# Interleaving two float32 tensors: transfer rows of 32 KiB instead of 16 KiB, with two buffers for each stream

## The chip, the cores and the metric

The kernel runs on one core of one Trainium2 chip. The metric is the device time of one launch in microseconds. Runs of one kernel mostly agree within about 0.3%.

A ratio below is the mean time of one kernel's fast runs over that of the kernel before in the same rounds on the same chip, so it is not quite the ratio of the medians that are quoted beside it.

## The reference

```python
batch, seq, dim = 32, 256, 1024           # x and y: float32, 33.6 MB each
result = np.zeros((batch, seq, dim * 2), dtype=np.float32)
result[..., 0::2] = x
result[..., 1::2] = y
```

No arithmetic is done. 67.1 MB are read and 67.1 MB written.

## The kernel before

Both inputs are treated as flat arrays and cut into tiles of 128 partitions x `WL` elements. SyncE issues the loads; VectorE copies x into the even columns and y into the odd columns of an output tile; ScalarE's queue issues the store. The tile list ends in a *taper*: smaller and smaller tiles. A *row* is the contiguous stretch that a transfer moves for one partition; the profile lists each row's move as a *packet*. An issue is the instruction that starts a transfer, a landing its end.

```python
WL = 4096          # load row: 4096 x 4 B = 16 KiB for each partition
WS = 2048          # store row: 2 x 2048 x 4 B = 16 KiB
xpool = ctx.enter_context(tc.tile_pool(name="xp", bufs=3))
ypool = ctx.enter_context(tc.tile_pool(name="yp", bufs=3))
opool = ctx.enter_context(tc.tile_pool(name="op", bufs=6))

lwidths = [WL] * (total // P // WL - 1) + [2048, 1024, 512, 256, 256]
for lw in lwidths:
    xtile = xpool.tile([P, WL], fp32, name="xtile")[:, :lw]
    ytile = ypool.tile([P, WL], fp32, name="ytile")[:, :lw]
    xs = dataclasses.replace(xf, offset=start, ap=[[lw, P], [1, lw]])
    ...
    nc.sync.dma_start(out=xtile, in_=xs)
    nc.sync.dma_start(out=ytile, in_=ys)
    soff = 0
    while soff < lw:
        width = min(WS, lw - soff)
        otile = opool.tile([P, 2 * WS], fp32, name="otile")[:, : 2 * width]
        ...
        nc.vector.tensor_copy(out=otile[:, 0::2], in_=xsub)
        nc.vector.tensor_copy(out=otile[:, 1::2], in_=ysub)
        nc.scalar.dma_start(out=os_, in_=otile)
        soff += width
    start += P * lw
```

## Time and profile before

| | kernel before |
|---|---|
| time, median of 4 | 319.75 us (319.66 to 320.22) |
| span in the profile | 317.6 us |
| bytes moved | 134.2 MB |
| VectorE busy | 24% of the span |
| 16.8 MB (eight transfers) in the steady part, called a *period* | 38.90 us, 431.3 GB/s |
| loads / stores | 40 / 35 |

The engines that move data are busy all the time, so the question for any change is only: at which rate do they run, and for how long are they not busy at the start and at the end? The prediction below shows the lines that say so. The period is read from the chain of waits, in order of time (start, length, what):

```profile
77.21 38.84 DMA xtile<-in_x_dram
...
116.11 38.84 DMA xtile<-in_x_dram
...
232.81 31.51 DMA xtile<-in_x_dram
```

(232.81 - 77.21) / 4 = 38.90 us. The texts on record have 38.89, from one window.

### The profile page before, as it was taken

The page shows a single profiled execution, that of the slowest core. Times are in us where ns is not written, and L with a number is a line of the kernel's source. Part 1 is how long each engine was busy: PE and PEld are TensorE (multiplying, and loading weights), DVE is VectorE, ACT ScalarE, POOL GpSimd, SP SyncE. Part 2 cuts the span into 40 slices and gives each one's busy share as a digit, 9 for nine tenths or more (in the row PEclk, how much of TensorE's full clock was granted, in tenths as well). Part 3 has the DMA queues.
Part 4 walks back from the last instruction along what each step waited for, and adds up shares of the span by engine and source line. Part 5 has one row for each costly group of instructions (what it writes and reads, how often), then busy time and mean ns, then how long its engine had stood idle before and what let it go on. Part 6 is the DMA issues. An engine that isn't in the chain of part 4 may idle for free.

```text
span 317.6 us, 285 instructions
## 1 busy us (share of the span) xinstructions
DVE 76.8 (24%) x70; POOL 0.2 (0%) x4
## 2 busy tenths in 40 slices
DVE  0522112222022221122220222202222202221130
POOL 0000000000000000000000000000000000000000
DMA  8999999999999999999999999999999999999997
GB/s 293 429 396 429 429 431 429 429 429 437 437 435 433 433 429 429 429 429 429 429 431 429 429 429 435 437 437 430 431 431 429 431 429 429 429 432 427 421 423 285
DMA packets 10802, 134.24 MB, mean 423 GB/s; under 512 B 1200, under 2 KB 1712, under 8 KB 2608
## 3 DMA queue, kind: packets, MB, share of 16 engines
q1 hardware_dynamic: 5760, 67.11, 50.0%
q10 hardware_dynamic: 5040, 67.11, 49.4%
q14 instruction: 2, 0.02, 0.0%
HBM read 67.11 MB, written 67.11 MB: 423 GB/s over the span
## 4 chain that ended last, share of the span: by engine, by line
DMA 94%; issue 3%; SPq 1%; DVE 1%
DMA xtile<-in_x_dram 82%; DMA ytile<-in_y_dram 12%; SPq L51 0%; DVE otile L69 0%; SPq L50 0%; DVE otile L68 0%
## 5 line engine op out<-in xcount | busy, mean ns | idle before, releaser
L68 DVE COPY otile<-xtile 128x2048 f32<-128x2048 f32 (+3 forms) x35 | 38.4, 1134 | 118.4 <-issue 94.4
L69 DVE COPY otile<-ytile 128x2048 f32<-128x2048 f32 (+3 forms) x35 | 38.4, 1134 | 117.9 <-DMA ytile<-in_y_dram 117.9
L90 POOL MEMSET const-bfloat16-1.0<- 128x1 bf16 x1 | 0.1, 102 | 0.0
L90 POOL MEMSET const-uint8-127<- 128x1 uint8 x1 | 0.1, 101 | 0.0
L90 POOL MEMSET const-float32-0.0<- 128x1 f32 x1 | 0.1, 99 | 0.2 <-issue 0.2
L90 POOL MEMSET const-float32-1.0<- 128x1 f32 x1 | 0.1, 98 | 0.0
## 6 DMA issues: line engine op xcount, KB each, us to landing
out_dram<-otile ACTq DMA_DIRECT2D x31, 2048.0 KB, 19.5
xtile<-in_x_dram SPq DMA_DIRECT2D x15, 2048.0 KB, 38.8
ytile<-in_y_dram SPq DMA_DIRECT2D x15, 2048.0 KB, 38.8
xtile<-in_x_dram SPq DMA_DIRECT2D x1, 1024.0 KB, 36.4
ytile<-in_y_dram SPq DMA_DIRECT2D x1, 1024.0 KB, 34.0
out_dram<-otile ACTq DMA_DIRECT2D x1, 1024.0 KB, 9.2
xtile<-in_x_dram SPq DMA_DIRECT2D x1, 512.0 KB, 29.0
ytile<-in_y_dram SPq DMA_DIRECT2D x1, 512.0 KB, 30.2
```

The lines of the kernel that those rows point to most:

```text
L68: nc.vector.tensor_copy(out=otile[:, 0::2], in_=xsub)
L69: nc.vector.tensor_copy(out=otile[:, 1::2], in_=ysub)
L90: nc = _bacc.Bacc("TRN2", target_bir_lowering=False, num_devices=1)
```

## The change

Its intent is to make all rows twice as long. The on-chip memory stays the same: 3 + 3 + 6 buffers of 16 KiB for each partition become 2 + 2 + 2 of 32 KiB, 192 KiB in both. The taper's pieces double as well.

```diff
-    WL = 4096
-    WS = 2048
+    WL = 8192
+    WS = 4096
@@
-    xpool = ctx.enter_context(tc.tile_pool(name="xp", bufs=3))
-    ypool = ctx.enter_context(tc.tile_pool(name="yp", bufs=3))
-    opool = ctx.enter_context(tc.tile_pool(name="op", bufs=6))
+    xpool = ctx.enter_context(tc.tile_pool(name="xp", bufs=2))
+    ypool = ctx.enter_context(tc.tile_pool(name="yp", bufs=2))
+    opool = ctx.enter_context(tc.tile_pool(name="op", bufs=2))
@@
-    lwidths = [WL] * (total // P // WL - 1) + [2048, 1024, 512, 256, 256]
+    lwidths = [WL] * (total // P // WL - 1) + [4096, 2048, 1024, 512, 512]
```

(A dead branch and an unused counter are removed too.)

More of the change, by code (lines that the diff above doesn't have):

```diff
@@ L33 @@
     fp32 = mybir.dt.float32
-    xpool = ctx.enter_context(tc.tile_pool(name="xp", bufs=3))
-    ypool = ctx.enter_context(tc.tile_pool(name="yp", bufs=3))
-    opool = ctx.enter_context(tc.tile_pool(name="op", bufs=6))
-    lwidths = [WL] * (total // P // WL - 1) + [2048, 1024, 512, 256, 256]
+    xpool = ctx.enter_context(tc.tile_pool(name="xp", bufs=2))
+    ypool = ctx.enter_context(tc.tile_pool(name="yp", bufs=2))
+    opool = ctx.enter_context(tc.tile_pool(name="op", bufs=2))
+    lwidths = [WL] * (total // P // WL - 1) + [4096, 2048, 1024, 512, 512]
     assert sum(lwidths) == total // P
     start = 0
-    k = 0
     for lw in lwidths:
@@ L63 @@
             ysub = ytile[:, soff : soff + width]
-            if False:
-                nc.gpsimd.tensor_copy(out=otile[:, 0::2], in_=xsub)
-                nc.gpsimd.tensor_copy(out=otile[:, 1::2], in_=ysub)
-            else:
-                nc.vector.tensor_copy(out=otile[:, 0::2], in_=xsub)
-                nc.vector.tensor_copy(out=otile[:, 1::2], in_=ysub)
+            nc.vector.tensor_copy(out=otile[:, 0::2], in_=xsub)
+            nc.vector.tensor_copy(out=otile[:, 1::2], in_=ysub)
             nc.scalar.dma_start(out=os_, in_=otile)
-            k += 1
             soff += width
```

## The prediction

> **What bounds the kernel now.** I read the page's first two parts, then the DMA groups, then a table of windows, then the chain of waits, and last what the load queue waited for.
>
> ```profile
> DVE 76.8 (24%) x70; POOL 0.2 (0%) x4
> ...
> DMA  8999999999999999999999999999999999999997
> GB/s 293 429 396 429 429 431 429 429 429 437 437 435 433 433 429 429 429 429 429 429 431 429 429 429 435 437 437 430 431 431 429 431 429 429 429 432 427 421 423 285
> DMA packets 10802, 134.24 MB, mean 423 GB/s; under 512 B 1200, under 2 KB 1712, under 8 KB 2608
> ...
> q1 hardware_dynamic: 5760, 67.11, 50.0%
> q10 hardware_dynamic: 5040, 67.11, 49.4%
> ```
>
> VectorE works a quarter of the span; the 16 DMA engines are busy in every slice, and the rate is flat except in the first and last slice. The packets tell how a row travels: 40 loads and 35 stores, each 128 rows plus 16 more, give 40 x 144 = 5760 and 35 x 144 = 5040. So a row is one packet, 16 KiB ones too.
>
> The windows (columns: stretch, length, VectorE busy, POOL busy, clock, DMA share, GB/s) give the rate of the steady part and of the edges:
>
> ```profile
> 3.00:8.46 5.46, 0.00 (x0) 0.00 (x0) 1.00 0.97 411
> ...
> 38.27:77.21 38.94, 9.46 (x8) 0.00 (x0) 1.00 1.01 431
> ...
> 288.70:296.00 7.30, 1.23 (x1) 0.00 (x0) 1.00 0.99 423
> 296.00:302.25 6.25, 1.23 (x1) 0.00 (x0) 1.00 1.00 421
> ...
> 312.70:315.00 2.30, 0.29 (x1) 0.00 (x0) 1.00 1.01 403
> 315.00:317.60 2.60, 0.00 (x0) 0.00 (x0) 1.00 0.15 55
> ```
>
> The chain of waits, in order of time (start, length, what), repeats one load every 38.9 us; its last load is tiny and slow:
>
> ```profile
> 38.31 38.84 DMA xtile<-in_x_dram
> ...
> 304.54 8.17 DMA ytile<-in_y_dram
> ```
>
> In a period of 38.89 us go eight transfers of 2.097 MB: 8 x 2.097 / 38.89 = 431.4 GB/s, or 4.86 us for each when alone. A load lands 38.8 us after its issue, eight times 4.86: four loads were in flight, each getting half the rate. That is a queue, not a latency. Hence the chain's 94% DMA means "the transport is full", not "a load comes late". The sum: 134.2 MB / 431.4 GB/s = 311.1 us of transport; the 2.57 MB moved by 8.46 us put its start at 2.5 us; the data ends about 315.3; then the last landing and the end, 2.3 us. That leaves 317.6 - 2.5 - 311.1 - 2.3 = 1.7 us lost, nearly all in the tail with its short rows. The measured time, 319.79, is 2.2 above the span.
>
> The load queue's own waits show that buffers are not the point:
>
> ```profile
> SPq L50 <- DMA xtile<-in_x_dram: 126.5, 14, 9.9
> SPq L51 <- DMA ytile<-in_y_dram: 121.9, 14, 9.4
> ```
>
> A load issue waits for an earlier load, not for a copy. The instruction order says why: completions are counted on eight semaphores in rotation, and in the steady part the x load of tile k must wait until that of tile k-2 has landed. The third x and y buffers are therefore scarcely used today; stores hold four of those semaphores.
>
> **What the Trainium skill says.** Four places, all on the page "DMA: Bandwidth & Descriptors". "Where 436 GB/s comes from" puts the ceiling of the 16 engines at 435 GB/s; the trace agrees, 431 in the steady part (single slices of 437 are packets booked in the slice in which they end). "Why small descriptors are slow (HBM only)" states a fixed overhead of about 3 cycles per packet; the trace agrees in direction, 421 to 423 GB/s where loads have rows of 8 and 4 KiB. "Queues, rings and completion order" says that each engine takes its queues in turn, one packet at a time; the trace agrees: the last y load, 128 KB, took 8.17 us, because each of an engine's 8 small rows waited behind a store's row. "Latency and other measured facts" reports that row pitches of 2 MiB and more in HBM cut the rate by a fifth to a half, and 512 KiB by only 3%; here the store pitch grows from 32 to 64 KiB, far below, and nothing in this trace shows such a loss.
>
> **The change part by part.** *Rows.* 24 loads and 19 stores in place of 40 and 35: (24 + 19) x 144 = 6192 packets instead of 10800. Per engine a 2.097 MB transfer is 8 rows, 131072 bytes, in 4861 ns; at the skill's ceiling it would be 4819. So at most 42 ns per transfer (5 ns a row) is overhead; doubled rows halve it: 21 of 4861, 0.43%, of 311.1 us = 1.3 us if all of the gap is per row or per transfer. It may be something else that does not halve; I take -0.9 us.
>
> *VectorE.* From 128x1024 at 695 ns and 128x2048 at 1225 ns the slope is 0.518 ns per element, so 128x4096 takes 1225 + 2048 x 0.518 = 2286 ns (estimate). 30 of these, 2 of 1225, 2 of 695 and 4 of 429 make 74.1 us instead of 76.8: beside the transport, worth nothing.
>
> *Start.* The first pair of loads is 8.4 MB instead of 4.2, so the first store is issued near 25 us instead of 14.6. But four loads, 16.8 MB or 39 us of transport, are issued at once, so the engines are full meanwhile: 0.
>
> *Steady part, with two buffers each.* I walk it with 9.72 us for a 4.194 MB transfer alone and 19.45 when shared. x0 lands at 8.46 + 4.86 = 13.3, y0 at 23.0, so store 0a is issued at 25.3 and 0b at 29.9. Sharing starts at about 26.8: x1 lands 38.7, y1 58.2, x2 77.6, y2 97.1, and stores 0a, 0b, 1a, 1b at 46.2, 65.7, 85.1, 104.6. Store 2a needs only y2's copy (its buffer came free at 85.1): issued 97.1 + 2.3 = 99.4, 5.2 us before 1b ends. The second half needs the buffer of 1b: copies 104.6 to 109.2, then store 2b is issued and y4's load too, x4's at 106.9, while x3 is in flight until 116.5 and y3 behind it. So the next period looks the same: the store queue is refilled 5.2 us (first half) and about 15 us (second half) ahead, and the load queue always holds a load or two. And should one run dry, the other takes the whole rate. Cost 0.
>
> *Tail.* Its pieces are twice as large, and only two output buffers are left. Continuing the walk, y6 lands near 252.7. Then loads with 16 and 8 KiB rows compete with 32 KiB store rows and get a third, then a fifth: x7 267.3, y7 281.9, x8 294.1; store 6b ends 286.5, store 7 298.7; y8 lands 300.2. Only loads are left then for some 4 us, just enough: y8's rest, x9, y9 and x10 are 1.5 + 1.2 + 1.2 + 0.6 us of work. Store 8 is issued at 301.5, runs from 303 to 308, and its buffer is what the copies of tile 10 wait for: about 309.4 with the landing. Store 9 fills until 310.4, store 10 begins near 311.8, tile 11's copies wait for store 9's landing, and the last store is issued near 312.8. The 256 KB last store of today lands in 3.2 us; one of 512 KB needs 0.6 more: 316.6, and 1.3 to the end of the span: 317.9. This is today's 317.6 + 0.3; the holes (some 1.4 us between stores 9 and 10, and 1 before 11) replace the losses of today's tail. I add 0.3 because such waits stack up late rather than early.
>
> *Sum.* 317.6 + 0.3 (tail) + 0.3 (its risk) - 0.9 (rows) = 317.3 of span; plus 2.2: 319.5 us.
>
> **Rivals.** First: two output buffers starve the store queue. For it: VectorE must wait for a store's landing before every copy, and refilling is only 5.2 us ahead. Against: stores share the engines with queued loads, so starving one queue costs nothing until both are empty. If both ran dry for 2 us in each of 7 periods: +14, 334. I give it 3%.
>
> Second: long rows move the HBM itself to another rate, by the pitch of 64 KiB or by turns between reading and writing 32 KiB at a time. For a gain: 423 to 431 from shorter to longer rows. Against: 431 is within 0.9% of the ceiling, so no more than 134.2/435.2 = 308.4 us can come of it, 2.7 less than now; the whole would be 317.1, not 2% faster. For a loss: nothing in this trace; 3% of loss would be 329. I give that 3%.
>
> Third: the tail with rows of 2 KiB behind rows of 32 KiB. Each engine's 8 rows of a small load can wait 8 x 1.2 = 9.7 us if a store of 32 KiB rows is in flight; if y8 or y9 lands after the stores have run out, the engines stand idle for the copy, the issue and the start of the next store, 3 us a time. For it: the 8.17 us above, and that my walk has only 0.3 us to spare at 303. Against: today's tail has the same proportions and lost under 2 us. It would make 321 to 323.
>
> **Range and chances.** The good end is the full row gain and today's tail, 318.2 or a little less; the bad end the third rival, 322.5. Range 317.7 to 322.5. Two per cent are 6.4 us: faster would need more than the ceiling leaves, slower one of the first two rivals. Faster 0.01, same 0.94, slower 0.05.
>
> **What would show it.** Right: 6194 packets; steady windows of 431 to 434 GB/s; 128x4096 copies near 2290 ns; a 4 MB load landing some 30 to 40 us after its issue; load issues waiting for copies or stores instead of earlier loads; the loss confined to the last 20 us. Wrong: a slice in the middle below 420 GB/s, both queues idle at once, a steady rate below 428, or packets split so that the count stays at 10800.

## The result, and the profile after

318.78 us (median of 4, 318.45 to 319.12) against 319.75; ratio 0.997, 95% interval 0.9956 to 0.9984. That is 0.3% faster: within 2%, clear of noise, and 0.7 us below the predicted 319.5.

The page of the changed kernel, its busy line, its rates and its packets:

```profile
DVE 73.5 (23%) x38; POOL 0.2 (0%) x4
...
GB/s 332 406 456 394 427 435 439 423 448 414 456 410 456 406 456 406 460 423 439 435 427 443 419 452 410 456 410 456 406 456 406 460 431 423 435 435 415 414 395 305
DMA packets 6192, 134.22 MB, mean 424 GB/s; under 512 B 688, under 2 KB 688, under 8 KB 1712
```

There are as many packets as rows again (24 x 144 + 19 x 144 = 6192), so a 32 KiB row goes as one packet. The rates now swing between 406 and 460. They mean nothing singly: a slice is 7.9 us and a row takes 1.2 us, so a slice can get up to one set of 16 rows (0.5 MB, 66 GB/s of a slice) more or less, one for each of the 16 DMA engines. Neighbouring slices average to 431 to 433. A better ruler is the spacing of like events in the chain of waits. Changed kernel, chain in order of time (start, length, what):

```profile
69.86 2.30 DVE otile L63
...
74.39 34.09 DMA out_dram<-otile
...
108.58 2.29 DVE otile L63
...
147.34 2.30 DVE otile L63
...
186.04 2.30 DVE otile L63
```

The spacing is 38.72 us (108.58 - 69.86), 38.76 and 38.70, where the kernel before had 38.90. The same 16.8 MB go through in 0.18 us less: 433.3 GB/s.

The chain also changed its names, from loads to stores. That is the new pacing by output buffers, and it looks alarming in the waits. Changed kernel, waits of VectorE and then of the load queue (engine, line, what it waited for: us in total, times, longest):

```profile
DVE otile L63 <- DMA out_dram<-otile: 180.6, 15, 23.2
DVE otile L64 <- DMA ytile<-in_y_dram: 35.5, 10, 7.6
```

```profile
SPq L49 <- DVE otile L63: 226.9, 10, 35.4
SPq L49 <- DMA xtile<-in_x_dram: 32.7, 8, 10.4
SPq L50 <- DVE otile L64: 19.5, 10, 4.5
```

VectorE now waits 180.6 us for stores to land, and loads wait 226.9 us for copies and 32.7 for loads; before, loads waited for loads. Yet the time fell. The waiting of VectorE, which is 23% busy, is free here as long as the transport always has a row to move, and it has: by the trace's packet records the store queue has no gap over 0.4 us until 298.9.

What is lost after the start is lost at the end. Windows of the changed kernel (stretch, length, VectorE busy, POOL busy, clock, DMA share, GB/s):

```profile
300.00:304.00 4.00, 2.45 (x3) 0.00 (x0) 1.00 0.94 360
304.00:308.00 4.00, 0.00 (x0) 0.00 (x0) 1.00 1.03 434
308.00:310.00 2.00, 0.76 (x2) 0.00 (x0) 1.00 1.02 422
310.00:312.00 2.00, 0.08 (x1) 0.00 (x0) 1.00 0.97 382
312.00:314.00 2.00, 0.73 (x2) 0.00 (x0) 1.00 0.72 295
314.00:316.30 2.30, 0.00 (x0) 0.00 (x0) 1.00 0.39 157
```

At 300 to 304 the stores have run out while y of the 2048 tile lands late (no store row moves from 298.9 to 302.8); at 310 to 314 the last copies wait for output buffers. In the timeline of the changed kernel (start, length, what, in brackets the idle time before it and what ended it):

```profile
299.83 1.23 DVE L64 COPY otile<-ytile 128x2048 f32<-128x2048 f32 x1 [7.58 <-DMA ytile<-in_y_dram]
...
308.87 0.43 DVE L63 COPY otile<-xtile 128x512 f32<-128x512 f32 x1 [5.79 <-DMA out_dram<-otile]
...
311.92 0.43 DVE L63 COPY otile<-xtile 128x512 f32<-128x512 f32 x1 [2.29 <-DMA out_dram<-otile]
```

### The profile page after: what moved, and what is told of

It is laid out like the page before. It is cut to its first block, busy times and chain, and to the rows that moved or that the text cites. A ratio compares the mean times of both kernels' runs of the same rounds, so it can differ in the third digit from the quotient of the medians.

```text
span 316.3 us, 179 instructions
## 1 busy us (share of the span) xinstructions
DVE 73.5 (23%) x38; POOL 0.2 (0%) x4
## 2 busy tenths in 40 slices
DMA packets 6192, 134.22 MB, mean 424 GB/s; under 512 B 688, under 2 KB 688, under 8 KB 1712
## 4 chain that ended last, share of the span: by engine, by line
DMA 89%; DVE 10%; issue 0%; SPq 0%; DVEq 0%
DMA out_dram<-otile 59%; DMA ytile<-in_y_dram 29%; DVE otile L64 6%; DVE otile L63 4%; SPq L49 0%; DVEq L63 0%
## 5 line engine op out<-in xcount | busy, mean ns | idle before, releaser
L63 DVE COPY otile<-xtile 128x4096 f32<-128x4096 f32 (+3 forms) x19 | 37.1, 1958 | 203.7 <-DMA out_dram<-otile 180.6
L64 DVE COPY otile<-ytile 128x4096 f32<-128x4096 f32 (+3 forms) x19 | 37.1, 1956 | 35.5 <-DMA ytile<-in_y_dram 35.5
## 6 DMA issues: line engine op xcount, KB each, us to landing
ytile<-in_y_dram SPq DMA_DIRECT2D x7, 4096.0 KB, 59.2
```

## The experiments

The theory after the result: each row costs a fixed few nanoseconds, so doubling rows gives about 8 x 0.18 = 1.4 us (134.2 MB are eight periods of 16.8 MB); the taper gives some tenths of it back; buffers play no part. Rivals: the overhead belongs to the transfer and not to the row; the gain comes from the buffers or the tail. The runs e1, e2, e6 and e7 went to one chip together, then e3, e4, e5 and e8, then e9 to e11.

### e1: one more, smaller piece in the taper

```diff
-    lwidths = [WL] * (total // P // WL - 1) + [4096, 2048, 1024, 512, 512]
+    lwidths = [WL] * (total // P // WL - 1) + [4096, 2048, 1024, 512, 256, 256]
```

> The changed kernel with its last tile of 512 split into 256 and 256, as the kernel before ends. Theory (the tail's larger last piece costs a few tenths, the rows gave about 1.4): ratio to the kernel before 0.996, the last store lands about 0.3 us earlier, about 318.4 us. Rival (the end is set by the wait for an output buffer's landing, of which this adds one more): the same as the changed kernel or 0.5 to 1 us slower, ratio 0.998 to 1.000.

Measured: 319.46 us (318.86 to 319.55), ratio 0.9985 (0.9973 to 0.9997). The 0.996 of my theory of the last piece lies outside the interval, so it fell. Against the changed kernel's 0.997 the run is about 0.5 us slower; the two intervals overlap, so the rival (the same or slower) held, and how much slower is not settled. Its timeline shows what a piece more brings:

```profile
309.36 0.43 DVE L63 COPY otile<-xtile 128x512 f32<-128x512 f32 x1 [6.01 <-DMA out_dram<-otile]
...
312.15 0.30 DVE L63 COPY otile<-xtile 128x256 f32<-128x256 f32 x1 [2.03 <-DMA out_dram<-otile]
...
313.99 0.29 DVE L63 COPY otile<-xtile 128x256 f32<-128x256 f32 x1 [1.35 <-DMA out_dram<-otile]
```

With two output buffers each of these pieces waits for a store to land. A piece more is a wait more, and the last copy starts 2.1 us later (313.99 against 311.92), though the piece is half the size.

### e2: the kernel before with two buffers each

```diff
-    ... bufs=3   (x)      ... bufs=3   (y)      ... bufs=6   (output)
+    ... bufs=2   (x)      ... bufs=2   (y)      ... bufs=2   (output)
```

> The kernel before with its 16 KiB rows, but two buffers each for x, y and output: a third of the on-chip buffer bytes goes for loads and two thirds for stores. Theory (the engines stay full as long as one of the two queues has work, so buffers are worth nothing in the steady part): steady period for 16.8 MB 38.9 us as before, ratio 1.000 to 1.005, what is lost only in the tail. Rival (two output buffers starve the stores, and the longer rows of the change hid this): both queues run dry, ratio 1.02 or more. If the theory holds, the gain of the change is not from its buffers.

Measured: 320.43 us (320.19 to 321.37), ratio 1.0025 (1.0013 to 1.0037). The chain of this run, in order of time:

```profile
51.65 16.93 DMA out_dram<-otile
...
71.10 16.93 DMA out_dram<-otile
```

One period here is one tile, half the bytes: 19.45 us, or 38.90 for 16.8 MB, as with three and six buffers. VectorE waits 222.7 us for stores, where the kernel before shows no such wait, and the steady rate does not notice. Half of the buffer memory brought nothing in the steady part. (In the run's expectation "goes" means "is taken away": x, y and output keep 32 KiB each, 96 of the former 192.) The 0.8 us lost lie outside the steady part; the timeline shows four store waits on the taper's copies. So the change's gain is not from its buffers, and its smaller number of buffers costs nothing in the middle.

### e6: 4 MiB transfers made of 16 KiB rows

```diff
-        xs = dataclasses.replace(xf, offset=start, ap=[[lw, P], [1, lw]])
+        # two chunks of memory: chunk c of partition p at start + c*P*4096 + p*4096
+        xs = dataclasses.replace(xf, offset=start, ap=[[4096, P], [P * 4096, 2], [1, 4096]])
```

(The same for y, and for the stores, whose rows of 16 KiB then lie in the two chunks; the copies take 2 x 2048 elements.)

> The changed kernel with its 4 MiB transfers and its buffers and tail, but each full transfer made of 256 rows of 16 KiB (two chunks of memory) in place of 128 rows of 32 KiB. Theory (some 5 ns of overhead for each row): period 38.9 us as in the kernel before, ratio 1.000 to 1.002, about 320.1 us. Rival (overhead of some 42 ns for each transfer, its completion, not each row): period 38.7 us as in the changed kernel, ratio 0.997. Packets will tell whether the rows really are 16 KiB: 272 for a full transfer.

Measured: 319.17 us (319.13 to 319.52), ratio 0.9984 (0.9972 to 0.9996). The page and the chain of this run:

```profile
DMA packets 9776, 134.22 MB, mean 423 GB/s; under 512 B 688, under 2 KB 688, under 8 KB 1712
```

```profile
97.66 29.72 DMA out_dram<-otile
...
136.53 29.72 DMA out_dram<-otile
```

9776 packets are the 6192 of the changed kernel plus 128 for each of the 14 full loads and 14 full stores (28 x 128 = 3584): the rows really are 16 KiB. The spacing is 38.87 us here and 38.88 over five periods. The steady part's gain is gone, though transfers, buffers and issues are those of the change. So 0.16 of the 0.18 us belong to the row; what a transfer costs besides is at most the 0.02 us between 38.88 and 38.90. This rests on the period: the total missed its 1.000 to 1.002, being 0.5 us better than the kernel before, and its interval overlaps that of the change. By the packet records of the two profiled runs the last row ends at 315.9 in this run and at 316.0 in the kernel before; most of the half microsecond lies after it (1.3 us to the end of the span against 1.7), and why is not known.

### e3 and e10: rows of 8 KiB and 4 KiB

```diff
-    WL = 4096         # e3: 2048      e10: 1024
-    WS = 2048         # e3: 1024      e10: 512
-    lwidths = [WL] * (total // P // WL - 1) + [2048, 1024, 512, 256, 256]
+    lwidths = [WL] * (total // P // WL - 2) + [2048, 1024, 512, 256, 256]   # e3
+    lwidths = [WL] * (total // P // WL - 1) + [512, 256, 256]               # e10
```

> The kernel before with all rows half as long (8 KiB, transfers of 1 MiB) in the steady part and the tail as before. Theory (a fixed 5.3 ns for each row on its engine): 16.8 MB take 16 x (2409 + 42) ns = 39.2 us in place of 38.9, over the whole run 2.7 us more, ratio 1.008, about 322.5 us. Rival (16 KiB rows were already at the limit of the engines and the 0.17 us per period of the change came from elsewhere): period 38.9, ratio 1.000. A threshold under which the rate falls faster would show as a ratio over 1.015.

> All rows of the steady part 4 KiB (transfers of 512 KiB), the tail the last pieces of the kernel before. Theory (5.3 ns for each row): 16.8 MB take 32 x (1205 + 42) ns = 39.9 us, over the whole run about 8 us more than the kernel before, ratio 1.025, about 328 us. Rival (short transfers also leave the engines idle between landing and the next issue, as only four loads and four stores can be open): ratio over 1.04.

Measured: e3 322.06 us, ratio 1.0077 (1.0064 to 1.0089); e10 328.86 us, ratio 1.0288 (1.0273 to 1.0302). The chain of e3, where each piece stands for 8.39 MB, and a window of e10:

```profile
23.94 19.56 DMA ytile<-in_y_dram
...
43.56 19.56 DMA ytile<-in_y_dram
```

```profile
117.00:156.00 39.00, 12.56 (x32) 0.00 (x0) 1.00 1.03 420
```

In e3 the spacing is 19.62 us for 8.39 MB, so 39.24 for 16.8 MB; in e10 16.78 MB at 420 GB/s take 39.95 (all seven windows read 420, rounded to 1 GB/s, so this is good to 0.05). With the other kernels:

| row | us for 16.8 MB | more than the row twice as long | one row in the trace's packet records, median |
|---|---|---|---|
| 32 KiB | 38.72 | | 1213 ns |
| 16 KiB | 38.90 | 0.18 | 611 ns |
| 8 KiB | 39.24 | 0.34 | 309 ns |
| 4 KiB | 39.95 | 0.71 | 159 ns |

Each halving about doubles the loss: a fixed cost for each row, with no threshold between 4 and 32 KiB. 16.8 MB are 32 rows of 32 KiB for each of 16 engines, 64 of 16 KiB, 128 of 8 KiB; 0.18 us / 32 more rows, 0.34 / 64 and 0.71 / 128 are 5.3 to 5.6 ns a row, about 5.5. (In e3 and e10 the transfers shrink with the rows, so up to a tenth of it may be the transfer's, by e6's 0.02 us.) The records themselves fit 8.5 ns + bytes / 27.2 GB/s. Successive records overlap (64 of 611 ns make 39.1 us, the period is 38.90), so only some 5.5 ns of the 8.5 count. Taking the overhead off (38.72 - 0.18 = 38.54 us) leaves 435 GB/s, which is the ceiling that the Trainium skill's page "DMA: Bandwidth & Descriptors" works out in "Where 436 GB/s comes from". The rest to be had beyond 32 KiB rows is thus an estimated 8 x 0.18 = 1.4 us.

### e4 and e5: long rows in one direction only

```diff
 e4:  WL = 8192, WS = 2048, buffers 2, 2 and 4   (loads 32 KiB, stores 16 KiB)
 e5:  WL = 4096, WS = 4096, buffers 3, 3 and 2   (loads 16 KiB, stores 32 KiB; one full tile less, for the longer taper)
```

> Loads with 32 KiB rows, stores with 16 KiB rows and four output buffers of half the size. Theory (every row costs the same, in either direction): half of the gain of the rows, period about 38.8 us per 16.8 MB; total ratio 0.997 to 1.000, its tail being another. Rivals: if only long loads help, 38.72; if only long stores help, 38.89.

> Loads with 16 KiB rows and three buffers each, stores with 32 KiB rows and two buffers. Theory: period about 38.8 us per 16.8 MB, the mirror of the run with long loads; total ratio 0.997 to 1.001. Since engines take the queues in turn by packet, stores get two thirds of the rate while they have work, so stores land sooner and their queue runs empty at times; the engines stay full with loads. Rivals: 38.72 if only long stores help; ratio above 1.003 if an empty store queue costs anything.

Measured: e4 321.11 us, ratio 1.0055 (1.0041 to 1.0069); e5 324.80 us, ratio 1.0169 (1.0145 to 1.0193). Both are misses: I expected half of the gain, and both lost. Windows of e5, with some of its middle and of its end, then its waits, and a piece of its chain:

```profile
134.00:174.00 40.00, 8.99 (x5) 0.00 (x0) 1.00 1.00 424
174.00:214.00 40.00, 8.86 (x5) 0.00 (x0) 1.00 1.01 424
...
315.00:320.00 5.00, 1.72 (x4) 0.00 (x0) 1.00 0.41 167
```

```profile
DVE otile L64 <- DMA ytile<-in_y_dram: 153.6, 18, 11.9
DVE otile L63 <- DMA xtile<-in_x_dram: 76.0, 17, 9.1
DVE otile L63 <- DMA out_dram<-otile: 15.9, 2, 11.6
```

```profile
94.97 19.09 DMA out_dram<-otile
...
114.13 46.59 DMA xtile<-in_x_dram
```

At the end, 3 us are lost in one stretch: the last loads land late (the last y load at 319.4, 21 us after its issue), and the last 5 us of loads and copies find too few stores to run beside (167 GB/s).

In the middle, the five windows from 54 to 254 us read 429, 427, 424, 424 and 423, on average 1.4% less than the 431.3 of 16 KiB rows alone, although a mix should lie between 431 and 433. The engines are not idle there. The rows take longer: by the packet records, what rows take above the median of their size, summed and divided by 16 engines, is 5.8 us in e5 and 3.4 in e4, against 1.8 in the kernel before and 1.8 in the changed one. From 30 to 285 us it is 3.65 us in e5 (1.4% of the stretch, the whole loss), 2.25 in e4 and at most 0.03 in the two others.

This excess sits where a queue that has run empty starts again. In e5 the store queue stands empty 15 times for over 1 us, and 3.2 us of the excess lie within 3 us of the ends of these gaps; in e4 it is the load queue, 6 times, for 7.6 to 11 us, with 1.4 us of excess. Equal rows show some of it too: in the kernel before, 0.6 us of its 1.8 lie where the first store joins the loads. So the records point to the restart, which e5's expectation had as its rival; no run tests it alone.

Why do the queues run empty? While both have work their rows alternate (e5, 160 to 171 us: 96 rows of each, stores 286 GB/s and loads 143), so the queue with the long rows finishes early. But a rival comes with the edit. Transfers count their completions on eight semaphores in rotation. In the kernel before and the changed one a steady load takes over the semaphore of an earlier load; with one store, or four, for two loads, it can take over that of a store. In e5 the x load at 114.13 uses that of the store issued at 94.97 and goes out right after this store has landed (94.97 + 19.09 = 114.06), though it needs neither its data nor its buffer; such waits of x loads for stores add up to 188.9 us in e5, and the changed kernel has none in its steady part. These two runs therefore do not show that unequal rows are costly in themselves, nor whether every row costs the same; they show that both kernels with unequal rows, as built, are slower than the kernel before and the changed one.

### e7 and e8: no taper

```diff
-    lwidths = [WL] * (total // P // WL - 1) + [ ... five small widths ... ]
+    lwidths = [WL] * (total // P // WL)          # e7: changed kernel; e8: kernel before
```

> The changed kernel without any small tiles at the end: eight tiles of 8192. Theory (loads run ahead and the store queue still holds some 7 us of work when the last y tile lands, so no taper is needed, and the taper's chain of small loads, copies and stores only makes holes): span about 315, ratio 0.992 to 0.995. Rival (the taper is needed to shorten the last copy and store): a hole of 3 us or more before the last 8 MB of stores, ratio 1.00 to 1.01.

> The kernel before without small tiles at the end: sixteen tiles of 4096. Theory (the taper costs more than it saves whatever the rows): 1.5 to 2 us less than the kernel before, ratio 0.994 to 0.996. Rival (only with 32 KiB rows and two output buffers does the taper cost, since only there its copies wait for stores to land): ratio 0.999 to 1.002.

Measured: e7 316.75 us (316.31 to 317.35), ratio 0.9906 (0.9893 to 0.9919). e8 318.47 us (318.35 to 318.85), ratio 0.9964 (0.9952 to 0.9977). The end of e7, timeline and then windows:

```profile
288.63 2.29 DVE L64 COPY otile<-ytile 128x4096 f32<-128x4096 f32 x1 [4.89 <-DMA ytile<-in_y_dram]
294.74 2.29 DVE L63 COPY otile<-xtile 128x4096 f32<-128x4096 f32 x1 [3.82 <-DMA out_dram<-otile]
```

```profile
295.00:300.00 5.00, 4.24 (x2) 0.00 (x0) 1.00 1.08 465
300.00:305.00 5.00, 0.00 (x0) 0.00 (x0) 1.00 1.02 439
```

The last y tile has landed at 288.6 and the last copy, right behind the one at 294.74, ends at 299.2, some 15 us before the end; from there on only stores are left and nothing in them waits for anything. No hole shows between 290 and 310. The taper guards against a long last copy and store, but the copy lies beside the store of the tile before, which is still running; what the taper adds is a chain of small loads that take turns with long store rows, and copies that wait for stores. It cost 0.36% in the kernel before and about 0.6% in the changed one, 1.1 and about 1.9 us. Part of this is again rows: the taper has eleven more transfers, 88 more rows for each engine, an estimated 0.5 us at 5.5 ns a row. How the rest divides between turns and waits is argued from the traces and not tested. The rival for e8, that only the new buffers make it costly, fell.

Without a taper the pair shows the rows nearly by themselves: 318.47 to 316.75, ratios 0.9964 and 0.9906, so 1.7 to 1.9 us; with e11 below in the place of e7 it is 1.3 to 1.6. The periods give 1.4.

### e9 and e11: the changed kernel and the version without taper on one chip

No edit: e9 is the changed kernel, e11 is e7 again.

> The changed kernel itself, unedited, to have it on one chip beside the version without small tiles. Theory: ratio to the kernel before 0.996 to 0.998, as at first.

> The changed kernel without small tiles once more, on the same chip as the changed kernel. Theory: ratio to the kernel before 0.990 to 0.992, so some 2 us less than the changed kernel in the same rounds. Rival (the earlier difference was between chips): within 0.5 us of the changed kernel.

Measured: e9 318.80 us (318.65 to 318.88), ratio 0.9973 (0.9959 to 0.9987). e11 317.13 us (316.29 to 317.31), ratio 0.9914 (0.9901 to 0.9927). Both repeat. The best version found is the changed kernel without small tiles: 0.9% faster than the kernel before, 0.6% faster than the change as made.

## Why the prediction was right

- **Bound.** Right. The transport is full before and after, and the waits that moved from loads to stores and copies did not matter in the steady part; e2 shows it apart from the rows.
- **Rows.** The mechanism was right, the size cautious. The text worked out at most 1.3 us and took 0.9; the periods show 8 x 0.18 = 1.4, the whole of it and a little more. It left open whether the row or the transfer is charged; e6 shows that it is the row.
- **VectorE.** 128x4096 copies were put at 2286 ns and took 2295 and 2292; 74.1 us in all were 73.5. Worth nothing, as said.
- **Start and steady part.** Right: cost 0. The first store was issued at 25.1 (25.3 predicted). The saying that a load lands 30 to 40 us after its issue was wrong, medians being 42.0 for x and 59.2 for y: the y load is issued 2 us after its x load but moves behind it, 4.2 MB in some 19 us, half of the rate. This had no part in the sum.
- **Tail.** The sum allowed 0.6 us. Landmarks came out close: y7 landed at 278.8 (281.9 predicted), y8 at 299.8 (300.2), the last store was issued at 312.8 (312.8). The walk's 4 us without stores (298.7 to 303) came at 298.9 to 302.8; the hole between stores 9 and 10 did not come, and the last store landed in 2.6 us, not 3.8. With 0.8 to 1.0 us of total gain (first runs and e9) and 1.4 from rows, some 0.4 to 0.6 were given back outside the steady part. The profiled pair, 1.3 us of span apart, gave back less: by the packet records its tail costs 0.7 us more up to the last row, the end after that 0.4 less (1.3 against 1.7) and the start 0.2 less.
- **Rivals.** Starved stores: fell (e2 with the change's buffer counts, and the steady period of the change itself). Another memory rate: fell, since four row lengths lie on one line up to the ceiling, with the pitch growing along with the row, and e6 lost the steady gain with 16 KiB rows. The slow tail: present, but small; y of the 2048 tile landed after the stores had run out, and this cost tenths of a microsecond, not 3.
- **A test of mine was badly chosen.** "A slice in the middle below 420 GB/s" was to show the prediction wrong; slices of 406 came, and they are only the booking of 16 rows at a time. The spacing of like events decides.
- **Two slips that did not matter.** The full row gain with today's tail is 317.6 - 1.3 + 2.2 = 318.5, not 318.2. And turns by row explain only part of the 8.17 us of the last y load: by the packet records its first row moves 3.3 us after the issue, and its rows then take 4.5 us; why it starts late is not shown.

Where did the expected gain of twice as long rows go? It was never large: at 16 KiB the rows' overhead was 2 x 1.4 us of 311.

## What to carry to other kernels

When the transport is full, count what is left by the spacing of equal events and compare it with the ceiling before lengthening rows: from 4 to 32 KiB the gain of each doubling was half of that of the one before. Large waits off the transport said nothing here, and half of the buffers brought nothing. Look at the ends: a taper of small tiles is a chain of dependent transfers, and it should be tried without. And when loads and stores get unequal sizes, look at what each issue waits for, since their order, their shares and their semaphores change together.

## What the Trainium skill lacked or had wrong

- "DMA: Bandwidth & Descriptors", section "Why small descriptors are slow (HBM only)": it gives the overhead as about 3 cycles per packet and speaks of sizes of 256 bytes. It lacks the cost at large rows: about 5.5 ns for each row from 4 to 32 KiB, so 420, 427.5, 431.3 and 433.3 GB/s with both directions running.
- The same page, section "Rules for kernel authors", asks for 1 MiB or more in a transfer for the most bandwidth. It lacks what size is worth in a queue that is never empty: 4 MiB with 16 KiB rows moved 16.8 MB in 38.88 us, 2 MiB with the same rows in 38.90, and transfers of 512 KiB, with 4 KiB rows, still gave 420 GB/s.
- No page that I read says what a queue's restart costs while the other queue runs: about 3.2 us of longer rows for 15 restarts in e5, where the cause is not tested; its middle gave 423 to 429 GB/s.
- No page that I read says what a taper of small last tiles costs: 0.36% and about 0.6% here.
